# Sum of reciprocals: the last 24 rows ordered op by op, shorter last loads, and a first load cut into parts

## The chip, the cores and the metric

The kernel runs on one core of a Trainium2 chip. The metric is the time of one execution on the device in microseconds (us). TensorE is called PE below, VectorE DVE, ScalarE ACT, GpSimd POOL; SP is the engine that issues the loads.

## What is computed

```python
def setup_inputs():
    batch, seq, dim = 32, 512, 1024
    return {"x": np.abs(np.random.randn(batch, seq, dim)).astype(np.float32) + 1e-6}

def reference(x):
    return np.sum(1.0 / x, axis=-1).astype(np.float32)
```

The 16384 vectors of 1024 numbers are laid out as 128 partitions with 128 rows each. "A row" below is one row on all 128 partitions: 128 x 1024 numbers, 0.5 MB, of which 128 sums come out. All of x is 67.1 MB.

## The kernel before

The kernel never takes the reciprocal of one number. A row has two halves a and b of 512 numbers, and 1/a + 1/b = (a + b) / (ab). So per row it makes one product ab of 512 numbers, then r = 1/(ab) as Exp(-Ln(ab)) on ACT (two activations), and then one of two sums on DVE:

- a plain row: one operation over 1024 elements multiplies a and b by r, read twice, and adds all up (`sum_row` with `row` and a broadcast `rc`);
- an "added" row: PE first adds the halves, with two matmuls by the identity into PSUM (`add`, tile `s`), and DVE then needs one operation over 512 elements only.

The product ab is made by POOL (line 144), mostly for two rows at a time. For some rows DVE makes it instead: PE copies b into PSUM (tile `b`), and DVE multiplies a by it (line 133).

Rows go through in chunks of two (or one), written (m, e, v): m rows, e of them added, v of them with the product on DVE. A is (2,0,0), B is (2,2,0), C is (2,2,1), L is (1,0,0), S1 is (1,1,0). The list LOADS says which chunks come in one load; a load is one DMA issued by SP into `ring`, which holds 40 rows. So the loads are eleven of 8 rows (A, B, A and B or C), six of 4 rows, and eight of 2 rows; of the last eight, five are one chunk of two rows and three are two chunks of one row.

For each chunk the order on the engines is: product, adds, then the DVE sums of the chunk before it (`sum_rows(*waiting)`), then Ln of the chunk, then Exp. `keep` pins the program order. The sums lag one chunk behind. A place in `ring` is free for the load 40 rows later when the DVE sum of its row is done (or, for an added row, when POOL and PE have read it). The pools: `ppool` holds 4 products for plain rows and 4 for added ones, `spool` 3 sums of halves, `bpool` one copy, `rpool` two results for plain rows. At the end SP stores `sums` (line 172).

A completion of a load is counted by one of eight semaphores, used in turn, so the ninth load waits for the completion of the first, and so on.

Of the kernel before, what the change touches and what calls it, by code (L numbers as in the profile page):

```python
# [1 line left out]

# [6 lines left out]


@with_exitstack
def kernel(
    ctx: ExitStack,
    tc: tile.TileContext,
    x: bass.AP,
    out: bass.AP,
):

    nc = tc.nc
    f32 = mybir.dt.float32
    P = 128  # L30
    D = 1024
    H = D // 2
    F = 128

    R = 40

    S = float(2**17)

    A, B, C = (2, 0, 0), (2, 2, 0), (2, 2, 1)
    L, S1 = (1, 0, 0), (1, 1, 0)
    LOADS = [[A, B, A, B], [A, B, A, C]] * 5 + [[A, B, A, C]]
    LOADS += [[A, B], [A, C]] * 3 + [[A], [B], [A], [B], [A]]
    LOADS += [[L, S1], [S1, S1], [L, S1]]

    Ln = mybir.ActivationFunctionType.Ln
    Exp = mybir.ActivationFunctionType.Exp
    mult = mybir.AluOpType.mult
    plus = mybir.AluOpType.add  # L50

    x_v = x.flatten_outer_dims().rearrange("(p f) d -> p f d", p=P)
    out_v = out.flatten().rearrange("(p f) -> p f", p=P)

    act_sets = list(get_activation_tables(nc.m.arch).keys())
    nc.scalar.add_instruction(  # L56
        mybir.InstLoadActFuncSet(
            name=nc.get_next_instruction_name(),
            act_func_set_id=act_sets.index("natural_log_exp_and_others"),
            ins=[],  # L60
            outs=[],
        )
    )

    ppool = ctx.enter_context(tc.tile_pool(name="ppool", bufs=4))
    opool = ctx.enter_context(tc.tile_pool(name="opool", bufs=1))
    spool = ctx.enter_context(
        tc.tile_pool(name="spool", bufs=3, space=bass.MemoryType.PSUM)
    )
    bpool = ctx.enter_context(  # L70
        tc.tile_pool(name="bpool", bufs=1, space=bass.MemoryType.PSUM)
    )
    rpool = ctx.enter_context(
        tc.tile_pool(name="rpool", bufs=2, space=bass.MemoryType.PSUM)
    )

    ring = opool.tile([P, R, D], f32)
    sums = opool.tile([P, F], f32)
    ident = opool.tile([P, P], f32)
    make_identity(nc, ident)  # L80
    keep = tc.keep_in_program_order

    def add(bank, *halves):
        for k, half in enumerate(halves):
            i = nc.tensor.matmul(  # L85
                bank,
                lhsT=ident,
                rhs=half,
                start=k == 0,
                stop=k == len(halves) - 1,  # L90
            )
            keep(i)

    def sum_row(c, row, fac, out=None):
        i = nc.vector.tensor_tensor_reduce(  # L95
            out=row if out is None else out,
            in0=row,
            in1=fac,
            scale=S,
            scalar=0.0,  # L100
            op0=mult,
            op1=plus,
            accum_out=sums[:, c : c + 1],
        )
        keep(i)

    def sum_rows(c, xc, pr, sm, rc):
        m, e = xc.shape[1], len(sm)
        for j in range(e, m):
            row = xc[:, j, :].rearrange("p (h e) -> p h e", h=2)  # L110
            sum_row(
                c + j,
                row,
                rc[j - e].unsqueeze(1).to_broadcast([P, 2, H]),
                pr[:, e : e + 2, :] if j == e and e + 1 < m else None,
            )
        for j in reversed(range(e)):
            sum_row(c + j, pr[:, j, :], sm[j])

    waiting = None  # L120
    c0 = 0
    for chunks in LOADS:
        n = sum(m for m, _, _ in chunks)
        xt = ring[:, c0 % R : c0 % R + n, :]
        keep(nc.sync.dma_start(out=xt, in_=x_v[:, c0 : c0 + n, :]))  # L125

        made, q = [], 0
        for m, e, v in chunks:
            pr = ppool.tile([P, m, H], f32, tag="ps" if e else "pr")
            for j in range(v):  # L130
                b = bpool.tile([P, H], f32, tag="b")
                add(b, xt[:, q + j, H:])
                i = nc.vector.tensor_tensor(  # L133
                    out=pr[:, j, :], in0=xt[:, q + j, :H], in1=b, op=mult
                )
                keep(i)
            made.append(pr)
            q += m

        q = 0  # L140
        for (m, e, v), pr in zip(chunks, made):
            xc = xt[:, q : q + m, :]
            if v < m:
                i = nc.gpsimd.tensor_tensor(  # L144
                    out=pr[:, v:, :], in0=xc[:, v:, :H], in1=xc[:, v:, H:], op=mult
                )
                keep(i)
            sm = []
            for j in range(e):
                s = spool.tile([P, H], f32, tag="s")  # L150
                add(s, xc[:, j, :H], xc[:, j, H:])
                sm.append(s)
            if waiting:
                sum_rows(*waiting)
            keep(nc.scalar.activation(out=pr, in_=pr, func=Ln, scale=S))  # L155
            rc = []
            if e < m:
                r = rpool.tile([P, m - e, H], f32, tag="rc")
                keep(
                    nc.scalar.activation(out=r, in_=pr[:, e:, :], func=Exp, scale=-1.0)  # L160
                )
                rc = [r[:, l, :] for l in range(m - e)]
            if e:
                r = pr[:, :e, :]
                keep(nc.scalar.activation(out=r, in_=r, func=Exp, scale=-1.0))  # L165
            waiting = c0 + q, xc, pr, sm, rc
            q += m
        c0 += n
    assert c0 == F, c0
    sum_rows(*waiting)  # L170

    nc.sync.dma_start(out=out_v, in_=sums)


# [1 line left out]
_INS = ['x']  # L176
_OUTS = [((32, 512), 'float32')]


# [23 lines left out]
```

## Time and profile before

| what | us |
|---|---|
| median of 9 runs (170.92 to 171.26) | 171.19 |
| the profiled execution | 171.25 |
| its span in the profile | 169.3 |

The time outside the span is 171.25 - 169.3 = 1.95 us. The profile's page lists busy time by engine, the span in 40 slices, the chain of work that ended last, and groups of instructions. A timeline lists instructions in order of time: start, duration, engine, line, operation, output and inputs, count, and in brackets the idle time before it and what ended it.

| engine | busy us | share of the span |
|---|---|---|
| POOL | 140.8 | 83% |
| ACT | 134.7 | 80% |
| PE | 131.0 | 77% |
| DVE | 121.1 | 72% |
| load queue (16 DMA engines) | | 93.1% |

### The profile page before, as it was taken

The page shows a single profiled execution, that of the slowest core. Times are in us where ns is not written, and L with a number is a line of the kernel's source. Part 1 is how long each engine was busy: PE and PEld are TensorE (multiplying, and loading weights), DVE is VectorE, ACT ScalarE, POOL GpSimd, SP SyncE. Part 2 cuts the span into 40 slices and gives each one's busy share as a digit, 9 for nine tenths or more (in the row PEclk, how much of TensorE's full clock was granted, in tenths as well). Part 3 has the DMA queues.
Part 4 walks back from the last instruction along what each step waited for, and adds up shares of the span by engine and source line. Part 5 has one row for each costly group of instructions (what it writes and reads, how often), then busy time and mean ns, then how long its engine had stood idle before and what let it go on. Part 6 is the DMA issues. An engine that isn't in the chain of part 4 may idle for free.

```text
span 169.3 us, 1265 instructions
## 1 busy us (share of the span) xinstructions
PE 131.0 (77%) x274; PEld 50.0 (30%) x274; DVE 121.1 (72%) x265; ACT 134.7 (80%) x135; POOL 140.8 (83%) x73
## 2 busy tenths in 40 slices
PE   0008999786988879875899869898879999997880
PEld 0003333231322333231343323243323434332320
DVE  0000777767987577776787689778789898988784
ACT  3002889978887988958979797898999999999992
POOL 1008999699995999769996998979999999999970
PEclk9999999999999999999789999999999999999997
DMA  6999999999999999999999999999999999999500
GB/s 217 410 457 410 457 410 457 410 457 403 457 404 457 410 457 406 449 412 441 418 449 418 449 418 435 399 426 432 430 426 426 430 412 420 418 424 422 238 0 15
DMA packets 3750, 67.24 MB, mean 397 GB/s; under 512 B 416, under 2 KB 544, under 8 KB 544
## 3 DMA queue, kind: packets, MB, share of 16 engines
q1 hardware_dynamic: 3744, 67.18, 93.1%
q8 instruction: 2, 0.03, 0.1%
q14 instruction: 4, 0.03, 0.0%
HBM read 67.11 MB, written 0.07 MB: 397 GB/s over the span
## 4 chain that ended last, share of the span: by engine, by line
DMA 52%; ACT 18%; POOL 16%; issue 7%; DVE 6%; DVEq 0%; POOLq 0%; SPq 0%
DMA ring<-in_x_dram 52%; POOL pr L144 16%; ACT pr L155 11%; ACT pr L165 4%; ACT r L160 3%; DVE ring L95 3%; DVE pr L95 2%; DVE pr L133 0%; DVE sums L95 0%; DVEq L198 0%; POOLq L144 0%; SPq L125 0%
## 5 line engine op out<-in xcount | busy, mean ns | idle before, releaser
L144 POOL TENSOR_TENSOR pr<-ring 128x1024 f32<-128x1024 f32 (+1 forms) x67 | 140.1, 2136 | 22.8 <-DMA ring<-in_x_dram 22.8
L85 PE MATMUL s<-ring,ident 128*128 128x512 f32 x256 | 122.9, 617 | 34.1 <-DMA ring<-in_x_dram 16.9
L155 ACT ACTIVATE pr<-pr 128x1024 f32<-128x1024 f32 (+1 forms) x67 | 67.9, 1013 | 28.5 <-POOL pr L144 28.5
L85 PEld LDWEIGHTS s<-ring,ident 128*128 128x128 f32 x256 | 46.7, 194 | 108.0 <-issue 61.0
L95 DVE CUSTOM_DVE_ANT_1 pr<-ring,r 128x1024 f32<-128x1024 f32 x31 | 37.9, 1221 | 44.7 <-ACT r L160 44.7
L95 DVE CUSTOM_DVE_ANT_0 pr<-pr,s 128x512 f32<-128x512 f32 x64 | 41.4, 683 | 0.0
L95 DVE CUSTOM_DVE_ANT_1 ring<-ring,r 128x1024 f32<-128x1024 f32 x33 | 40.1, 1217 | 0.6 <-issue 0.6
L165 ACT ACTIVATE pr<-pr 128x1024 f32<-128x1024 f32 (+1 forms) x34 | 34.2, 1007 | 1.1
L160 ACT ACTIVATE r<-pr 128x1024 f32<-128x1024 f32 (+1 forms) x33 | 33.1, 1002 | 1.0
L95 DVE DVE_READ_ACCUMULATOR2_ANT sums<- 128x1 f32 x128 | 10.6, 83 | 0.0
L85 PE MATMUL b<-ring,ident 128*128 128x512 f32 x18 | 10.5, 668 | 0.0
L133 DVE TENSOR_TENSOR pr<-ring,b 128x512 f32<-128x512 f32 x9 | 6.1, 683 | 0.5 <-PE b L85 0.5
L85 PEld LDWEIGHTS b<-ring,ident 128*128 128x128 f32 x18 | 3.3, 202 | 6.2 <-DMA ring<-in_x_dram 4.6
L56 ACT ACT_TABLE_LOAD x1 | 1.3, 1283 | 0.7 <-PEq L187 0.7
masks.py:197 POOL MEMSET ident<- 128x128 f32 x1 | 0.2, 205 | 0.3 <-POOLq L187 0.3
masks.py:199 POOL TENSOR_SCALAR_AFFINE_SELECT ident<-ident 128x128 f32<-128x128 f32 x1 | 0.3, 293 | 0.1
L187 POOL MEMSET const-float32-0.0<- 128x1 f32 x1 | 0.1, 98 | 0.2 <-issue 0.2
L187 POOL MEMSET const-bfloat16-1.0<- 128x1 bf16 x1 | 0.1, 103 | 0.0
L187 POOL MEMSET const-uint8-127<- 128x1 uint8 x1 | 0.1, 103 | 0.0
L187 POOL MEMSET const-float32-1.0<- 128x1 f32 x1 | 0.1, 99 | 0.0
## 6 DMA issues: line engine op xcount, KB each, us to landing
ring<-in_x_dram SPq DMA_DIRECT2D x11, 4096.0 KB, 37.8
ring<-in_x_dram SPq DMA_DIRECT2D x6, 2048.0 KB, 36.8
ring<-in_x_dram SPq DMA_DIRECT2D x8, 1024.0 KB, 28.2
out_dram<-sums SPq DMA_DIRECT2D x1, 64.0 KB, 1.5
```

Of the source, the lines that this page charges most:

```text
L56: nc.scalar.add_instruction(mybir.InstLoadActFuncSet(name=nc.get_next_instruction_name(), act_func_set_id=act_sets.index("natural_log_exp_ ...
L85: i = nc.tensor.matmul(bank, lhsT=ident, rhs=half, start=k == 0, stop=k == len(halves) - 1,)
L95: i = nc.vector.tensor_tensor_reduce(out=row if out is None else out, in0=row, in1=fac, scale=S, scalar=0.0, op0=mult, op1=plus, accum_out ...
L133: i = nc.vector.tensor_tensor(out=pr[:, j, :], in0=xt[:, q + j, :H], in1=b, op=mult)
L144: i = nc.gpsimd.tensor_tensor(out=pr[:, v:, :], in0=xc[:, v:, :H], in1=xc[:, v:, H:], op=mult)
L155: keep(nc.scalar.activation(out=pr, in_=pr, func=Ln, scale=S))
L160: nc.scalar.activation(out=r, in_=pr[:, e:, :], func=Exp, scale=-1.0)
L165: keep(nc.scalar.activation(out=r, in_=r, func=Exp, scale=-1.0))
L187: nc = _bacc.Bacc("TRN2", target_bir_lowering=False, num_devices=1)
```

## The change

There are two parts.

First, the end. The loads of 8 rows become ten (rows 0 to 79), the six of 4 rows stay (80 to 103), and the last 24 rows (104 to 127) come in ten loads of 2 rows and four of 1 row. What is done with these 24 rows is written out in the list ORDER, one operation after the other: P a product on POOL, D one on DVE from the ring, B and V a copy by PE and the product on DVE from it, S the two adding matmuls, L and E the Ln and Exp, T the sum on DVE; the number is the row, and a plus means that row and the next in one instruction. Rows 109, 114, 121 and 123 have their product on DVE. All other rows keep the general loop, where the first load's chunks are now B, B, A, A.

Second, the first load (rows 0 to 7). Rows 4 to 7 come in one DMA from SP. Rows 0 to 3 come in eight parts: part k is partitions k, k+8, k+16 and so on, 16 of them. Parts 1 to 7 are one DMA each from SP, issued after that of rows 4 to 7. Part 0 is two DMAs of eight partitions from POOL's queue, and ahead of each of these goes a DMA of one number for each of eight partitions into a tile `spare` that nothing reads. With these, the loads of SP's queue number eight before that of rows 8 to 15, which therefore waits for rows 4 to 7.

```diff
     A, B, C = (2, 0, 0), (2, 2, 0), (2, 2, 1)
-    L, S1 = (1, 0, 0), (1, 1, 0)
-    LOADS = [[A, B, A, B], [A, B, A, C]] * 5 + [[A, B, A, C]]
-    LOADS += [[A, B], [A, C]] * 3 + [[A], [B], [A], [B], [A]]
-    LOADS += [[L, S1], [S1, S1], [L, S1]]
+    LOADS = [[B, B, A, A], [A, B, A, C]] + [[A, B, A, B], [A, B, A, C]] * 4
+    LOADS += [[A, B], [A, C]] * 3
+    LAST = 104
+    LAST_LOADS = [2] * 10 + [1] * 4
+    ORDER = """
+        P104+ P106 L104+ S109 P107 E104 E105 T104 P108 B109 L106 L107 S107
+        V109 E106 P110+ T105 L108+ E107 S110 T106 E109 P112+ E108 T107 L110+
+        T108 E110 B114 T109 P115 E111 T110 L112+ S114 V114 E112 T111 L114+
+        P116+ S115 T112 E113 E114+ T113 S117 L116 P118+ T114 L117 T115 E116
+        S118 E117 T116 L118+ P120 T117 S119 E118+ D121 L120+ T118 B123 P122
+        T119 E120+ S122 V123 P124 L122 T120 L123 P125 L124 S124 T121 E122 E123
+        P126 T122 E124 S126 T123 L125 P127 L126 T124 E125 S127 E126 T125 L127
+        E127 T126 T127
+    """
...
+    spare = opool.tile([P, 1, 1], f32)
...
+    def first_load(xt, n):
+        h = n // 2
+        for g in range(0, P, P // 2):
+            for dst, rows, w in ((spare, 1, 1), (xt, h, D)):
+                at = slice(g, g + P // 2, 8)
+                keep(
+                    nc.gpsimd.dma_start(
+                        out=dst[at, :rows, :w], in_=x_v[at, :rows, :w]
+                    )
+                )
+        keep(nc.sync.dma_start(out=xt[:, h:, :], in_=x_v[:, h:n, :]))
+        for k in range(1, 8):
+            at = slice(k, P, 8)
+            keep(nc.sync.dma_start(out=xt[at, :h, :], in_=x_v[at, :h, :]))
...
-        keep(nc.sync.dma_start(out=xt, in_=x_v[:, c0 : c0 + n, :]))
+        if c0 == 0:
+            first_load(xt, n)
+        else:
+            keep(nc.sync.dma_start(out=xt, in_=x_v[:, c0 : c0 + n, :]))
...
+    c0 = LAST
+    for n in LAST_LOADS:
+        xt = ring[:, c0 % R : c0 % R + n, :]
+        keep(nc.sync.dma_start(out=xt, in_=x_v[:, c0 : c0 + n, :]))
+        c0 += n
     sum_rows(*waiting)
+    for op in order:
+        kind, c, n = op[0], int(op[1:].rstrip("+")), 1 + op.endswith("+")
+        j = (c - LAST) % 2
+        rows = ring[:, c % R : c % R + n, :]
+        a, b = rows[:, :, :H], rows[:, :, H:]
+        pr = None if kind in "WX" else pair(c)[:, j : j + n, :]
+        if kind == "P":
+            keep(nc.gpsimd.tensor_tensor(out=pr, in0=a, in1=b, op=mult))
+        elif kind == "D":
+            keep(nc.vector.tensor_tensor(out=pr, in0=a, in1=b, op=mult))
...
+        elif kind == "L":
+            keep(nc.scalar.activation(out=pr, in_=pr, func=Ln, scale=S))
...
```

## The prediction

> **What bounds the kernel now.** I read the page's slices first, then POOL's timeline, then the DMA view of the last loads, then the timeline after them.
>
> ```profile
> span 169.3 us, 1265 instructions
> POOL 1008999699995999769996998979999999999970
> DMA  6999999999999999999999999999999999999500
> q1 hardware_dynamic: 3744, 67.18, 93.1%
> ```
>
> The DMA row is full from the second slice to the 37th: 93.1% of 169.3 us is 157.6 us of loading without a gap. The stream of loads sets the pace, at one row per 1.22 us (by the completion events of the trace, 8-row loads land 9.71 us apart, 4-row loads 4.89, 2-row loads 2.45).
>
> ```profile
> 13.46 9.32 POOL L144 TENSOR_TENSOR pr<-ring 128x1024 f32<-128x1024 f32 x4 [12.15 <-DMA ring<-in_x_dram]
> 23.13 8.26 POOL L144 TENSOR_TENSOR pr<-ring 128x1024 f32<-128x1024 f32 x4 [0.35 <-DMA ring<-in_x_dram]
> ...
> 102.77 8.27 POOL L144 TENSOR_TENSOR pr<-ring 128x1024 f32<-128x1024 f32 x4 [0.70 <-DMA ring<-in_x_dram]
> 112.14 52.05 POOL L144 TENSOR_TENSOR pr<-ring 128x1024 f32<-128x1024 f32 x27 [1.11 <-DMA ring<-in_x_dram]
> ```
>
> POOL, the busiest engine, waits for a load in front of each 8 rows: four products cost 9.32 us, or 8.26 with one row on DVE, against 9.71 of loading. Only from 112.14 on does it run through, 52.05 us, to 164.19. But the last load lands at 161.19 and its two products of 1.28 would end at 163.8 in any case, so POOL adds 0.4 us to the loads' end, no more.
>
> ```profile
> core 0 of [0], span 169.3 us
> DMA  9999797989999698999745332131212100000000
> GB/s 468 374 468 468 328 515 328 468 375 421 468 421 515 281 468 374 468 375 468 328 187 234 140 140 94 47 140 47 94 47 94 47 0 0 0 0 0 0 0 0
> ```
>
> This is the DMA view of 155 to 162 us, 0.175 us a slice. The load does not end at once: from 158.7 the row falls to a few tenths. Of the last load's 16 completions thirteen come from 158.82 to 159.84, and three at 161.06, 161.06 and 161.19. The trace shows six fetches of instructions among the loads (from 47.5 to 140.8 us), and after each one engine's completions come about 1 us later for good.
>
> ```profile
> 163.05 0.63 ACT L165 ACTIVATE pr<-pr 128x512 f32<-128x512 f32 x1
> 163.59 0.61 ACT L155 ACTIVATE pr<-pr 128x512 f32<-128x512 f32 x1
> 164.23 0.60 ACT L160 ACTIVATE r<-pr 128x512 f32<-128x512 f32 x1
> 164.77 0.61 ACT L155 ACTIVATE pr<-pr 128x512 f32<-128x512 f32 x1
> 165.41 0.63 ACT L165 ACTIVATE pr<-pr 128x512 f32<-128x512 f32 x1
> ```
>
> After the last landing come two products, Ln, Exp and a DVE sum (166.11); the sums are complete at 166.80, 5.61 us after the landing. The store then takes to 169.3, which the change leaves alone.
>
> [...]
>
> **The change part by part.**
>
> *POOL's work at the end.* Rows 104 to 127 had, before, 8 products of two rows and 7 of one: 8 x 2.33 + 7 x 1.28 = 27.6 us. Now 20 rows are on POOL, 5 of two and 10 of one: 5 x 2.33 + 10 x 1.28 = 24.5 us, while loading takes 24 x 1.22 = 29.3. It saves 3.1 us on an engine that the loads hold back, so worth nothing beyond the 0.4 above: POOL now waits for loads again. DVE gets three more products than before in these rows (4 x 0.6 against 1), in all 12 added sums x 0.6 + 12 plain x 1.14 + 4 x 0.6 = 23.3 us of 29.3. ACT needs 24 x 1.04 to 1.15, some 26. All fit, ACT the tightest.
>
> *The tail, step by step.* Take the last landing where it was, 161.19. The four last rows land singly, 1.22 apart: 124 at 157.5, 125 at 158.75, 126 at 159.97. POOL is released for row 122 at 156.3 and then runs singles of 1.28: 122, 124, 125, 126, 127 end at 157.6, 158.9, 160.2, 161.4 and 162.7. ACT: row 120's product ends at 155.15; D121 runs beside it[...]. From there ACT has the pair 120+ (2 x 1.04) and twelve singles at 0.57 (in the rows above a Ln and an Exp together take 1.18, and two Ln in sequence wait less for each other): 2.08 + 6.84 = 8.92 us, ending at 164.1 to 164.8. By POOL alone it could not end before about 164.4: L126 at 161.4, then E125, E126, L127, E127, five times 0.57 with starts. Then T127, 0.61 with its read: sums complete at 165.0 to 165.5. I take 165.3, a gain of 166.80 - 165.3 = 1.5 us. The waits that take the place of the old ones are Exp's own: ACT is late next, no longer POOL.
>
> *Smaller descriptors.* The packets of before take 1.213 us for 32 KB, 0.612 for 16 KB, 0.312 for 8 KB; so about 0.011 us each are fixed. Replacing one 8-row load by 4 rows in twos and 4 singly: 9.9 us (the singles by extrapolation 1.25 each) for 9.71, +0.19. The first load in 16 KB pieces: 8 x 0.011, +0.09. Together +0.28 on the path, since nothing covers the stream.
>
> *The first load's order.* The first product (rows 0 and 1) needs all eight parts, which SP issues behind rows 4 to 7. So it starts when 4.2 MB have come, as now (13.46): the parts bring nothing forward, but a later or earlier POOL start costs nothing either while loads are waited for. SP issues 8 DMAs at about 0.55 (five took 2.89): done by 5.2. The load of rows 8 to 15 waits for rows 4 to 7, which land near 8.0 to 8.6; behind it on SP wait only the next loads, released by parts landing within the next 4 us. Its own first packet follows 1.0 us after issue (0.74 to 1.75 for the first load), at 9.6, and the parts keep the rings busy to about 12: covered by 2.4 us. POOL's four DMA issues stand before its first product with 12.15 idle us: hidden.
>
> *Which engines carry part 0.* Each engine used to have 8 pieces of 16 KB of rows 0 to 3;[...] at 0.61 us a piece. If all three late engines are among the relieved, the last landing is 0.6 earlier; if one is among the loaded, 0.6 later. The profile does not name the engines. I take 0, ends -0.6 and +0.6.
>
> *How fast the parts go.* Nearest row: 16 KB in 0.612. Below that no reason. Above:[...] each piece takes twice as long, and 7 x 0.61 = 4.3 us more pass before the stream goes on. If the DMA engine's own pace (32 KB in 1.213) is the limit,[...] nothing. I take nothing, and keep 4.3 as the end.
>
> *Sum.* -1.5 + 0.28 = -1.2 us on the profiled 171.25, so 170.05; the median is 0.06 lower: 170.0.
>
> **Rivals.**
>
> 1. Late engines relieved: 170.0 - 0.6 = 169.4. For it: three engines alone hold the last 1.3 us, so there is something to shift. Against: nothing shows that they are in the same half.
> 2. Slower: the parts at half rate.[...] In full 170.0 + 4.3 = 174.3, half of it 172.1. It decides once the parts lose over 1.2 us, that is below 4.3/5.5 = 78% of full rate.
> 3. The tail keeps its length:[...] a buffer wait holds ACT, for 1.2 us in the last 8 rows: 171.2. For it: ACT's 26 us of 29.3 leave little room. Against: the plan above leaves POOL 1 us of wait before row 122.
> 4. A gap in the stream after the first load, if the release of rows 8 to 15 comes over 3.6 us later than reckoned: above 171.5.
>
> **How the numbers follow.** My forecast 0.40, rival 1 0.20, rival 2 0.27 (0.15 in full, 0.12 in part), rival 3 0.08, rival 4 0.05. Faster by over 0.2% (0.34 us, about what a measurement of this kernel can tell from no change): 0.60. Within: 0.08. Slower: 0.32. The forecast's own range with rival 1 is 168.9 to 170.8; to leave out no more than 2 in 10 it must reach into the slower cases, to 173.6, short of the full half rate (0.15).
>
> **What would show it.** Right: POOL's first product near 13.5; loads landing 9.71 apart from there; waits of POOL for loads in the last 24 rows; ACT unbroken from about 155.5; sums complete about 4.4 us after the last landing. Wrong: the second load landing over 24.5 (parts slow, or a gap: the DMA row of the first 14 us tells which), or ACT or POOL waiting for DVE in the tail.

## The result, and the profile after

| | before | after |
|---|---|---|
| median, us | 171.20 (29 runs) | 176.95 (9 runs, 176.13 to 177.49) |
| span of the profiled execution | 169.3 | 175.3 |
| first POOL product starts | 13.46 | 20.90 |
| rows 8 to 15 landed | 23.06 | 30.44 |
| last load landed | 161.19 | 168.61 |
| sums complete | 166.80 | 172.66 |

The ratio is 1.0339, 95% interval 1.0326 to 1.0351: slower by 5.75 us. (Landings are the last of the 16 completions of a load in the trace.) Single executions that came slow, most of them 2 to 3 us above the rest of their run, are left out of the ratios, and the profile of the column parts below is of such a one, so its span is not compared.

These are the lines of the page of after that answer to those shown of before.

```profile
span 175.3 us, 1331 instructions
POOL 6000299988999699976999699999999999979780
DMA  6999899999999999999999999999999999999800
GB/s 213 329 202 239 288 464 434 404 464 404 449 441 398 464 404 441 445 404 443 426 434 441 419 436 400 434 426 417 430 426 430 409 424 419 421 419 416 351 25 17
q1 hardware_dynamic: 4688, 66.91, 93.6%
```

The GB/s row of before:

```profile
GB/s 217 410 457 410 457 410 457 410 457 403 457 404 457 410 457 406 449 412 441 418 449 418 449 418 435 399 426 432 430 426 426 430 412 420 418 424 422 238 0 15
```

The DMA row looks as full as before, and this is the trap. The GB/s row says what the full queues moved: 202, 239 and 288 GB/s in the third to fifth slice, where before had 457, 410 and 457. Here a packet counted as busy although it moved slowly: by the trace's packets a 16 KB piece took 1.2 us between 12 and 17 us, against the 0.61 of before. So there is no gap in the stream; it runs at half its rate between about 7 and 20 us. The view of windows says it in one number (columns: stretch, its length, busy time and count of PE, PEld, DVE, ACT, POOL, PE clock, DMA share, GB/s):

```profile
7.00:20.20 13.20, 0.00 (x0) 0.00 (x0) 0.00 (x0) 0.00 (x0) 0.00 (x0) 1.00 1.05 225
20.20:60.00 39.80, 34.83 (x69) 14.69 (x70) 27.08 (x59) 32.04 (x31) 35.48 (x17) 0.96 1.00 431
```

POOL's timeline of after starts 7.4 us late and then has the rhythm of before; at the end it waits for loads again:

```profile
20.90 9.29 POOL L183 TENSOR_TENSOR pr<-ring 128x1024 f32<-128x1024 f32 x4 [17.14 <-DMA ring<-in_x_dram]
30.51 8.28 POOL L183 TENSOR_TENSOR pr<-ring 128x1024 f32<-128x1024 f32 x4 [0.31 <-DMA ring<-in_x_dram]
...
156.31 6.25 POOL L237 TENSOR_TENSOR pr<-ring 128x1024 f32<-128x1024 f32 x3 [1.17 <-DMA ring<-in_x_dram]
163.77 6.31 POOL L237 TENSOR_TENSOR pr<-ring 128x512 f32<-128x512 f32 x5 [1.20 <-DMA ring<-in_x_dram]
```

And the tail on ACT, which had been L, E, L, E with one row each after the last two products:

```profile
168.48 1.13 ACT L255 ACTIVATE pr<-pr 128x512 f32<-128x512 f32 x2
169.52 0.58 ACT L261 ACTIVATE r<-pr 128x512 f32<-128x512 f32 x1
170.04 0.61 ACT L261 ACTIVATE pr<-pr 128x512 f32<-128x512 f32 x1
170.56 0.61 ACT L255 ACTIVATE pr<-pr 128x512 f32<-128x512 f32 x1
171.20 0.63 ACT L261 ACTIVATE pr<-pr 128x512 f32<-128x512 f32 x1
```

From the last landing to the complete sums it is now 172.66 - 168.61 = 4.05 us instead of 5.61. So the two parts of the change pull apart in the trace already: the loads end 7.42 us later, what follows them is 1.56 us shorter, and 7.42 - 1.56 = 5.86 is the difference of the sums' ends.

### The profile page after: what moved, and what is told of

Read it like the earlier page. It is cut to its first block, busy times and chain, and to the rows that moved or that the text cites. A ratio compares the mean times of both kernels' runs of the same rounds, so it can differ in the third digit from the quotient of the medians.

```text
span 175.3 us, 1331 instructions
## 1 busy us (share of the span) xinstructions
PE 132.3 (75%) x278; PEld 52.8 (30%) x278; DVE 122.6 (70%) x268; ACT 134.0 (76%) x143; POOL 140.2 (80%) x77
## 4 chain that ended last, share of the span: by engine, by line
DMA 67%; ACT 9%; PE 7%; POOL 5%; DVE 5%; SPq 3%; issue 2%; DVEq 0%; POOLq 0%; ACTq 0%
DMA ring<-in_x_dram 67%; PE s L102 7%; ACT pr L255 5%; POOL pr L183 4%; ACT pr L261 2%; SPq L154 2%; DVE pr L112 2%; ACT r L261 2%; POOL pr L237 1%; DVE ring L112 1%; PE bb L102 0%; DVE pr L246 0%; DVE pr L172 0%; SPq L151 0%; DVE sums L112 0%
## 5 line engine op out<-in xcount | busy, mean ns | idle before, releaser
L183 POOL TENSOR_TENSOR pr<-ring 128x1024 f32<-128x1024 f32 (+1 forms) x52 | 112.8, 2201 | 26.0 <-DMA ring<-in_x_dram 26.0
L194 ACT ACTIVATE pr<-pr 128x1024 f32<-128x1024 f32 x52 | 54.7, 1053 | 33.4 <-POOL pr L183 33.3
L112 DVE CUSTOM_DVE_ANT_1 pr<-ring,r 128x1024 f32<-128x1024 f32 x27 | 32.9, 1220 | 17.2 <-ACT r L199 17.2
L112 DVE CUSTOM_DVE_ANT_1 ring<-ring,r 128x1024 f32<-128x1024 f32 x37 | 44.8, 1216 | 0.2 <-issue 0.2
L204 ACT ACTIVATE pr<-pr 128x1024 f32<-128x1024 f32 x26 | 27.5, 1057 | 0.8
L199 ACT ACTIVATE r<-pr 128x1024 f32<-128x1024 f32 x26 | 26.7, 1028 | 1.6 <-DVE sums L112 0.8
L237 POOL TENSOR_TENSOR pr<-ring 128x512 f32<-128x512 f32 (+1 forms) x15 | 24.4, 1645 | 3.2 <-DMA ring<-in_x_dram 2.7
L255 ACT ACTIVATE pr<-pr 128x512 f32<-128x512 f32 (+1 forms) x17 | 13.1, 794 | 1.1 <-DVE pr L246 0.8
L261 ACT ACTIVATE pr<-pr 128x512 f32<-128x512 f32 (+1 forms) x10 | 6.9, 704 | 0.1
L261 ACT ACTIVATE r<-pr 128x512 f32<-128x512 f32 (+1 forms) x11 | 6.8, 625 | 0.1
L102 PE MATMUL bb<-ring,ident 128*128 128x512 f32 x6 | 3.2, 622 | 1.3 <-DMA ring<-in_x_dram 1.2
L246 DVE TENSOR_TENSOR pr<-ring,bb 128x512 f32<-128x512 f32 x3 | 2.1, 686 | 0.9 <-PE bb L102 0.8
```

What stands on the lines that cost most here:

```text
L102: i = nc.tensor.matmul(bank, lhsT=ident, rhs=half, start=k == 0, stop=k == len(halves) - 1,)
L112: i = nc.vector.tensor_tensor_reduce(out=row if out is None else out, in0=row, in1=fac, scale=S, scalar=0.0, op0=mult, op1=plus, accum_out ...
L183: i = nc.gpsimd.tensor_tensor(out=pr[:, v:, :], in0=xc[:, v:, :H], in1=xc[:, v:, H:], op=mult)
L237: keep(nc.gpsimd.tensor_tensor(out=pr, in0=a, in1=b, op=mult))
L246: nc.vector.tensor_tensor(out=pr[:, 0, :], in0=a[:, 0, :], in1=bs[c], op=mult)
L261: keep(nc.scalar.activation(out=r, in_=pr, func=Exp, scale=-1.0))
```

## The experiments

A piece is one packet of 16 KB, four rows of one partition. Theory P: its time goes by which partitions are being loaded, not by the queue or by the number of DMAs. The traces of before and after have 0.61 us with all partitions and 1.2 with 16 eight apart; that 16 neighbours would take twice as long again was supposed, and no trace had shown it. The rivals put the loss into waits and many small DMAs (I), POOL's queue (W), or the memory's side (H).

**One part at a time.** The new end alone is the changed kernel with

```diff
-        if c0 == 0:
-            first_load(xt, n)
-        else:
-            keep(nc.sync.dma_start(out=xt, in_=x_v[:, c0 : c0 + n, :]))
+        keep(nc.sync.dma_start(out=xt, in_=x_v[:, c0 : c0 + n, :]))
```

> The change with its first load whole again, in one DMA (only the new end is left). All theories put the loss into the first load's parts, so this gives the size of the new end by itself: load of rows 8 to 15 lands at about 23.1 us as before, last landing 161.3 to 161.6, sums complete 4.05 us after it as in the changed kernel: 165.5 on the profile's clock for 166.80 before, so 171.2 - 1.3 = 169.9 us (169.6 to 170.2). If the new end were itself at fault for a part of the loss, it would be 171.2 or more.

The new first load alone is `first_load` put into the kernel before:

> The kernel before with the new first load alone. Theory P ([...]pieces take twice as long or more): the whole stream is 7.3 us late, 171.2 + 7.3 = 178.5 us, first POOL product at 20.9 us. Rival: the loss needs both parts of the change (the new end's waits reach back): then less than 176.9.

Measured: the end alone 170.09 us, ratio 0.9948 (0.9933 to 0.9964); rows 8 to 15 landed at 22.97. The first load alone 178.56 us, 1.0414 (1.0383 to 1.0446); rows 8 to 15 landed at 30.43 and POOL started here:

```profile
21.13 17.65 POOL L167 TENSOR_TENSOR pr<-ring 128x1024 f32<-128x1024 f32 x8 [17.36 <-DMA ring<-in_x_dram]
```

The whole loss, and more, is the first load's: +7.5 us on the median of 171.09 that ran beside it (with the new end it is 176.95 - 170.09 = 6.9). The end gains 1.0, where 1.3 was expected, and the rival that needs both parts is out.

**The same DMAs, all partitions.** Rows 0 to 3 in eight parts again, but each is half a row on all partitions:

```diff
-        for k in range(1, 8):
-            at = slice(k, P, 8)
-            keep(nc.sync.dma_start(out=xt[at, :h, :], in_=x_v[at, :h, :]))
+        parts = [(slice(r, r + 1), slice(g, g + H)) for r in range(h) for g in (0, H)]
+        for k, (r, g) in enumerate(parts):
...
+                keep(nc.sync.dma_start(out=xt[:, r, g], in_=x_v[:, r, g]))
```

> The changed kernel with the same number of DMAs for rows 0 to 3 and the same bytes in each, but each part is half a row on all 128 partitions (2 KB pieces) instead of four rows on 16 partitions; the first part comes from POOL's queue, seven from SP behind rows 4 to 7. Theory P:[...] the stream runs at full rate, with 56 more descriptors per engine at about 0.011 us: 169.9 + 0.6 = 170.5 us (170.0 to 171.0). Rival I (many small DMAs, and the load of rows 8 to 15 that waits for rows 4 to 7, leave a gap): as the changed kernel, 176 to 177 us.

Measured: 170.63 us, 0.9977 (0.9962 to 0.9992); rows 8 to 15 landed at 23.26, and from 9 to 17 us the stream moved 444 GB/s. Number and bytes of the parts' DMAs, the wait of the next load and its issue behind eight others on SP are there, and the loss is gone. Rival I is out. The 0.54 us above the whole load agree with what the small descriptors were reckoned at, 0.6.

**Neighbours.** Parts of 16 neighbouring partitions; part 0 is one DMA from POOL's queue, and the spare copies are gone (the diff leaves both out):

```diff
...
-            at = slice(k, P, 8)
+            at = slice(16 * k, 16 * k + 16)
```

> The changed kernel with parts of 16 neighbouring partitions (16k to 16k+15) instead of every eighth; part 0 in one DMA from POOL's queue, no spare.[...] Theory P: a piece takes 4 x 0.61 = 2.4 us instead of 1.2, the eight parts take up to 19.5 us instead of 4.9: 169.9 + 12 to 15 = 182 to 185 us. Rival H (the loss is on the memory's side, partitions eight apart are 4 MB apart in x): neighbouring partitions are no slower than in the changed kernel: 176.9 us or less. Rival I (small DMAs, waits): 176 to 177 us.

Measured: 183.50 us, 1.0711 (1.0678 to 1.0744), in the range of P. Side by side (columns as in the view of windows above), the stretch from 9 to 17 us with all partitions (the run with two halves, below), with every eighth, all from SP (next), and with neighbours, in this order:

```profile
9.00:17.00 8.00, 8.00 (x16) 3.10 (x14) 1.30 (x4) 5.67 (x6) 7.81 (x4) 1.00 1.04 446
```
```profile
9.00:17.00 8.00, 0.00 (x0) 0.00 (x0) 0.00 (x0) 0.00 (x0) 0.00 (x0) 1.00 1.05 231
```
```profile
9.00:17.00 8.00, 0.00 (x0) 0.00 (x0) 0.00 (x0) 0.00 (x0) 0.00 (x0) 1.00 1.00 170
```

446, 231, 170 GB/s; the last stretch still has pieces of rows 4 to 7 in it. The packets say the same: a 16 KB piece took 0.61 us with all partitions, 1.26 with every eighth and 1.92 with neighbours (medians). Neighbours should have been helped or left alone if partitions 4 MB apart in x were the trouble; rival H is out in this form. Another form stays open, in all the runs: x gives every partition its own 0.5 MB, so a part's partitions and its addresses in x go together, and a limit of the memory that goes by these addresses would give the same times. The runs show which parts are slow; whether the side that is read or the side that is written makes them so was not shown.

One size is off: the neighbours' parts from SP landed 1.9 us apart, not 2.4. That the total fell in P's range all the same is luck in part: rows 4 to 7 landed here only at 13.12, against 8.40 where all parts come from SP, and why was not tested.

**Without POOL's queue, and without the spare copies.** In one run all eight parts come from SP, and the DMAs of POOL's queue are gone (the first diff leaves this out); in another the `spare` copies alone are left out:

```diff
...
-        for k in range(1, 8):
+        for k in range(8):
```

> The changed kernel with all eight parts, every eighth partition, from SP, and nothing from POOL's queue. Theory P: every engine has 8 pieces at 1.22 us, 4.9 us more than at full rate: 169.9 + 4.9 = 174.8 us (174.3 to 175.6), near the run without the spare copies. Rival W (POOL's DMAs slow the rings): at most 171 us.

```diff
-            for dst, rows, w in ((spare, 1, 1), (xt, h, D)):
+            for dst, rows, w in ((xt, h, D),):
```

> The changed kernel without the two spare copies. Theory P[...] the two groups of completions 2.4 us apart in the first load become one group, the first product starts at 18.5 to 19.5 instead of 20.9, and the time is 174.7 to 175.7 us. Rival W (the DMAs from POOL's queue themselves slow the rings): two of four gone, and the pieces get faster than 1.2 us. Rival C[...]: groups and time stay as they are, 176.9 us.

Measured: all from SP 174.66 us, 1.0194 (1.0174 to 1.0215), POOL starting at 18.21; no spare copies 175.73 us, 1.0266 (1.0251 to 1.0280), starting at 19.45:

```profile
18.21 9.29 POOL L170 TENSOR_TENSOR pr<-ring 128x1024 f32<-128x1024 f32 x4 [16.90 <-DMA ring<-in_x_dram]
```
```profile
19.45 9.31 POOL L182 TENSOR_TENSOR pr<-ring 128x1024 f32<-128x1024 f32 x4 [16.75 <-DMA ring<-in_x_dram]
```

Rival W is not the bulk: with nothing on POOL's queue 4.6 of the 6.9 us lost stay. But the queue adds to it, and so do the spare copies: in the changed kernel the completions of part 7 come in two groups of eight, 17.40 to 18.02 and 20.02 to 20.73, two pieces apart; without the spare copies they are one, 18.39 to 19.28.

**The order alone.** The run with all parts from SP showed an uneven step. Its parts landed (first engine) at 8.91, 10.19, 11.44, 12.66, 13.56, 14.85, 16.14 and 17.39: 1.22 to 1.29 us apart, but 0.90 from part 3 to part 4. I changed only the order, so that every step goes between parts 0 to 3 and parts 4 to 7:

```diff
-        for k in range(8):
+        for k in (0, 4, 1, 5, 2, 6, 3, 7):
```

> The run with all eight parts from SP, with one thing changed: the parts are issued in the order 0, 4, 1, 5, 2, 6, 3, 7 instead of 0 to 7.[...] In the run in order the parts landed 1.25 us apart, and only from part 3 to part 4 was it 0.9. Theory P: all steps become 0.9 or less, the eight parts take about 2.4 us less: 174.7 - 2.4 = 172.3 us (171.3 to 173.3). Any other theory (memory's side, size or number of DMAs, waits, queues): 174.7 us as before, since nothing but the order differs.

Measured: 173.46 us, 1.0137 (1.0124 to 1.0150). The parts landed at 8.69, 9.71, 10.75, 11.80, 12.85, 13.91, 14.96, 16.04: steps of 1.02 to 1.08 us, and a piece took 1.05. The stretch from 9 to 17 us rises from 231 to 258 GB/s:

```profile
9.00:17.00 8.00, 0.00 (x0) 0.00 (x0) 0.00 (x0) 0.00 (x0) 0.00 (x0) 1.00 1.00 258
```

That is 1.2 us off the time for an order of the same DMAs (1.0 against the kernel before that ran beside each; rows 8 to 15 landed 0.99 earlier, 26.70 against 27.69). The step was expected at 0.9, and the time came 0.16 above its range, so P has the direction and not the size. Of the theories named, the direction fits P alone; the form of H left open above would give it too.

**Does an earlier start count?** The first load in two DMAs of four rows, all partitions, in place of the parts:

```diff
...
+        keep(nc.sync.dma_start(out=xt[:, :h, :], in_=x_v[:, :h, :]))
+        keep(nc.sync.dma_start(out=xt[:, h:, :], in_=x_v[:, h:n, :]))
```

> The change with its first load in two DMAs of four rows on all partitions, rows 0 to 3 first. POOL then starts its first product at about 8.5 us instead of 13.5. My prediction's step that an earlier start brings nothing while POOL waits for loads: same as the run with the whole first load, within 0.2 us. Rival: the start counts: up to 4 us faster.

It came 0.5 us below the whole load: 169.57 us, 0.9894 (0.9874 to 0.9914), against 170.09. The two had run on different chips, so both were run again on one, with the two lines above swapped as a third:

> The same kernel as the run with the new end and the whole first load, again, beside the next two: 169.6 to 170.1 us.

> The same kernel as the run with rows 0 to 3 first, then 4 to 7, again. In its trace the last landing was 0.10 us earlier than with the whole first load, and the rest of its 0.5 us was one DVE sum that started 0.49 us after its Exp had ended. If an earlier start of POOL brings nothing, it is 0.1 to 0.5 us faster than the whole load and equal to the swapped halves; if the start counts, it is faster than the swapped halves.

> Two DMAs for the first load as in the run before, but rows 4 to 7 first, so that POOL starts at about 13.2 us instead of 8.3. If the start brings nothing: within 0.2 us of rows 0 to 3 first. If the start counts: slower by more than that, like the whole load.

Measured: whole 170.09 us, 0.9947 (0.9934 to 0.9961); rows 0 to 3 first 169.51, 0.9908 (0.9895 to 0.9921); rows 4 to 7 first 169.51, 0.9905 (0.9890 to 0.9919). POOL's first product in the two halved runs:

```profile
8.15 4.66 POOL L168 TENSOR_TENSOR pr<-ring 128x1024 f32<-128x1024 f32 x2 [6.85 <-DMA ring<-in_x_dram]
```
```profile
13.12 9.29 POOL L168 TENSOR_TENSOR pr<-ring 128x1024 f32<-128x1024 f32 x4 [11.82 <-DMA ring<-in_x_dram]
```

Five microseconds of start make no difference. What the halves gain over the whole is not the start. Of the 0.63 us between the ends of the sums, the last landing gives 0.27 (161.45 against 161.18); in the rest one DVE sum plays a part, in the whole load's run only:

```profile
163.38 1.22 DVE L111 CUSTOM_DVE_ANT_1 ring<-ring,r 128x1024 f32<-128x1024 f32 x1 [0.36 <-issue]
```

It starts 0.49 us after its Exp ended (162.89), in both runs of that kernel; in the halved run the same sum starts 0.13 us after its Exp. The profile names no cause, and it stays open. The halves with the new end are the fastest version seen, 1.6 us below the kernel before.

**Single loads without the new order.** The kernel before with its last loads cut:

```diff
-    LOADS += [[L, S1], [S1, S1], [L, S1]]
+    LOADS += [[L], [S1], [S1], [S1], [L], [S1]]
```

> The kernel before with its last three loads of two rows cut into six of one row, the order of work as it was. If POOL's 3.1 us saved and the order op by op carry the gain at the end, cutting the loads alone gives next to nothing, because POOL runs through from 112.14 to 164.19: 171.2 us (171.0 to 171.4). If the single loads carry it, 169.9 us.

Measured: 171.91 us, 1.0038 (1.0020 to 1.0055), with 22 runs that spread from 171.21 to 173.39. No gain; it is even 0.6 us slower, which the expectation did not allow. POOL, as expected, runs through to the end:

```profile
111.75 52.59 POOL L144 TENSOR_TENSOR pr<-ring 128x1024 f32<-128x1024 f32 x27 [1.12 <-DMA ring<-in_x_dram]
```

It ends at 164.34. The last load itself landed at 162.00, 0.8 later than before, and why was not pursued; one product of 1.28 after it would have ended at 163.3, so POOL is 1.0 us behind the loads here.

## Why the prediction was wrong

*The failed step is "How fast the parts go".* It had two ends, nothing and 4.3 us, and took nothing, because the DMA engine's own pace might have been the limit. What sets the pace is which partitions a part has: the stretches with parts of every eighth partition moved 225 GB/s in the change and 231 with all parts from SP, those with full loads 431 to 446. Rival 2 was the right one, and the prediction gave it 0.27. No load of before reaches only some of the partitions, so its trace could not tell the two ends apart, and that was not a reason to take the favourable one.

*The worse end was too good as well.* The range stopped at 173.6, short even of the prediction's own worse end, 174.3, and the loss was larger than that end. By the landing of rows 8 to 15 the loss divides like this:

| step | landed | added |
|---|---|---|
| two halves, all partitions | 22.78 | |
| eight parts of every eighth partition, all from SP | 27.69 | 4.91 |
| part 0 from POOL's queue instead | 28.94 | 1.25 |
| with the spare copies (the change) | 30.44 | 1.50 |

(The two runs of the whole first load landed rows 8 to 15 at 22.97 and 23.13, so 0.2 us in these steps means nothing.) The first is the doubled piece, now for 8 pieces where 4.3 counted 7. The third is the prediction's "which engines carry part 0", mis-sized: it stood at ±0.6 us, one piece at full rate. The two groups of completions begin 20.02 - 17.40 = 2.62 us apart, about two pieces at half rate, 2 x 1.2 = 2.4 us; without the spare copies the one group begins between them, at 18.39. So the later group is about one piece late: 1.2 reckoned so, 1.50 measured. The two steps multiply, and the sum had added them. For the second, the trace of after has pieces from POOL's queue of up to 1.8 us beside rows 4 to 7 and part 1; why they are that slow was not tested.

*Which engines carry part 0* was not shown. That the spare copies load some engines more than others was supposed: the two groups with them, and the one without, agree with it, but the completions do not name an engine. Rival 1, late engines relieved, had no chance to show under the rest.

*The tail* was right: a gain of 1.5 us after the last landing was predicted, 1.56 measured in the change; with the end alone it was 1.24 in both runs, where one DVE sum starts 0.36 us late. ACT is unbroken there, and POOL's waits are 1.17 and 1.20 where 1 was reckoned. D121 took 0.87 us:

```profile
162.24 0.87 DVE L239 TENSOR_TENSOR pr<-ring 128x512 f32<-128x512 f32 x1
```

POOL's product beside it ended at 162.56, 0.32 us after D121 began, which leaves 0.55. In the ten other traces of the new end the overlap is 0.30 to 0.32, once 1.20 (the column parts), and D121 less the overlap is 0.55 each time. By these numbers it waited for POOL's product to end, which cost DVE 0.3 us.

The expected 170.0 us is near what the end alone gives, 170.09; the prediction's own terms for the end, -1.5 and +0.19, make 169.9. That single loads alone do not bring it is what the run with single loads shows. The prediction's "worth nothing beyond the 0.4" was right for the kernel as it stood and wrong as a judgement of what the single loads need, where POOL was 1.0 us behind. How much of the gain is POOL's saved time and how much the order op by op, no run separates.

*Descriptors,* +0.28 on the path: the column parts agree with their size (0.54 us for 2 KB pieces, 0.6 reckoned). *No gap* in the stream: right, although the load of rows 8 to 15 was issued at 11.59 instead of 8 to 8.6, since the slow parts covered it. *The start counts for nothing:* right, by the swapped halves.

*Three readings were slightly off* and did not matter: loads of two rows land 2.48 us apart, and only the last pair 2.44; the sum puts 4.1 us between the last landing and the sums (165.3 - 161.19), not the 4.4 named as a sign; and SP's eight DMAs were issued by 6.09, not 5.2.

## What to carry to other kernels

Judge a load by the partitions that it reaches, not only by its bytes and its descriptors: here both a strided and a neighbouring set of 16 slowed the whole stream that was queued behind it (231 and 170 GB/s from 9 to 17 us, against 446 with all partitions). Read the GB/s row beside the DMA row, since the DMA row was as full at 225 GB/s as at 431. Where the stream of loads is the bound, look at what stands between the last landing and the end: 5 us of earlier start brought nothing here, the new end 1.0 us.

## What the runs showed that I had not expected

The order of the parts counts: in the order 0, 4, 1, 5, 2, 6, 3, 7 they went at 1.05 us a step instead of 1.25, though each part has the same 16 partitions in both orders. The runs show no cause for it, and none for the 1.9 us between the parts of neighbouring partitions, where 4 x 0.61 = 2.4 was supposed.

And the six instruction fetches in the trace of before were not alike, where the prediction put each at about 1 us: after each of the four of 8 KB one engine's completions come 0.6 to 1.0 us later for good, after each of the two of 16 KB 1.5 us. Two of 16 KB, and two of 8 KB on one engine, account for the three engines that end over a microsecond behind the other thirteen. (The events do not name the engines; each is told by its constant place among the 16 completions.)
